# The tile transposed ahead, in more pieces: root, scaling with transposition, and each modulation by itself

## The chip, the cores and the metric

The kernel runs on one core of one Trainium2 chip. The metric is the device time of one execution in microseconds; the median of the runs is what counts. A core has five engines, each with its own queue of instructions that it works through in order: TensorE (PE, matrix products; PEld is its weight load), VectorE (DVE), ScalarE (ACT), GpSimd (POOL) and SyncE (SP), which here only issues DMA transfers (SPq in the rows). Engines wait for each other by semaphores.

## What is computed

One inference step of a hybrid decoder layer in float32: 2048 prompt tokens and 8 sample tokens, model width 1024. Cut to what matters here:

```python
ada = silu(c) @ w_ada + b_ada
shift, scale, gate = split(ada, 3)
hn = rmsnorm(x, g_norm) * (1.0 + scale) + shift
xa, za, q, k, v, glr, zg = split(hn @ w_in, SPLITS)
y_lru = rg_lru(conv4(xa)) * silu(za)
y_gla = rmsnorm(gla_chunked(q, k, v, decay(glr)), g_gla_norm) * silu(zg)
x = x + gate * (concat([y_lru, y_gla]) @ w_out)
y = rmsnorm(x, g_final)
```

`rmsnorm` scales a token's row by the inverse root of its mean square. The recurrence `rg_lru` has two sigmoid gates, each a block-diagonal product of the convolution's result; `gla_chunked` is a gated linear attention with 4 heads in chunks of tokens, whose running state passes from chunk to chunk.

## The kernel before

**Products.** Every float32 operand is kept as a high part (cast by ScalarE) and a low part (the rest, a subtraction on VectorE), and a product is three matmuls. A token tile is 128 tokens; the prompt is worked in two halves of 1024 tokens (`TH`). The normalised and transposed activations of a half lie in `hh` and `hl`.

**Stages of the first half.** The four heads run in the order 3, 0, 1, 2. For each, `values` makes the values in 8 token tiles (matmuls L388 to L390, 192 in all; ScalarE casts the high part at L999, VectorE makes the low part at L1000). Then come k and q (L703 to L705), the decay (matmul L1015, ScalarE L1020 to L1054, VectorE L1021 to L1051), the two decayed operands (L1063 for k, L1069 for q), their transposition on PE (L1084, L1087), and the chunks: VectorE L1088 to L1094, PE L1110 to L1118, the running state L1120 and L1121, the result copied out at L1124. ScalarE sums its squares (L167), VectorE takes the root and scales it (L1132), PE transposes it (L1206), VectorE multiplies by the silu gate (L1211; the silu itself is made at L1172 and L1173). Between the chunks run tiles of the recurrent group: convolution (ScalarE L1319, VectorE L1321), its high and low part (L1345, L1346), the two gates on PE (L1358 to L1360), their sigmoids (L1361), decay (L1366 to L1369) and recurrence (L1373 to L1377, results at L1395). Four accumulators of PE (`acc`) are shared by all of it, so PE can begin a fifth group only when the first has been read.

**Work for later, between these.** `weights` loads a piece of `w_in` (L340, two buffers), casts it (ScalarE L346), makes the low part (VectorE L347) and stores the pair for the second half (L364). `pair_weights` makes combinations of weights (VectorE L819, four a pair, then ScalarE L824 and VectorE L825). `out_weights` does the like for the output projection (L852 to L907). And `turn_ahead(q, gm)`, q from 0 to 7, makes the input of the second half: it loads 128 rows of the prompt (L266), ScalarE sums the squares of each row (L167, 128x1024), VectorE takes the inverse root in twelve small operations (L149 to L155), scales the rows (L183, 128x1024), transposes the tile in 32x32 blocks (L277, two of 128x512), multiplies by the modulation's scale and adds its shift (L284, twice 128x1024), and SyncE stores the result in four parts to `fd` (L289). `x` (the rows) and `w` (the transposed tile) share two buffers of one tag, `xt`. When one tile is stored, the next is started, so tile q+1 is loaded when tile q is done.

**What sets the order.** The program runs on a logical clock: `tick` is called once per block of matmuls, and `after(units, fn)` puts a piece of work on a heap, due that many ticks later; `tick` runs what is due. `behind(V)` makes the instructions of a piece follow VectorE's last one so far. In `turn_ahead` the square comes 3 ticks after the load; root, scaling and transposition together half a tick later; both modulations half a tick later; the stores half a tick later. The tile framework's scheduler then fixes the order on each engine from the program's order, the dependences and its own estimate of durations, so the order of an engine's queue is not the order of the code, and a piece that moves by a tick can change which instructions of other stages stand before it.

Of the kernel before, what the change touches and what calls it, by code (L numbers as in the profile page):

```python
# [8 lines left out]
F32 = mybir.dt.float32  # L9
# [3 lines left out]
OP = mybir.AluOpType  # L13

P = 128
D = 1024
KT = D // P
T = 2048
TH = T // 2
NS = 8  # L20
# [34 lines left out]
def hybrid_kernel(ctx, tc, i, o):  # L55
    nc = tc.nc
    V, S, G, PE, SP = nc.vector, nc.scalar, nc.gpsimd, nc.tensor, nc.sync
# [30 lines left out]
    xp = p1.enter_context(tc.tile_pool(name="xp", bufs=2))  # L88
# [52 lines left out]
                    mybir.DependencyClass.NoSync, mybir.DependencyReason.DATA), reason="in_order")  # L141
            last[x.engine] = x

    def rsqrt(pool, out, ss, n, rows, scale):

        y = pool.tile([P, 16], F32, tag="rs_y", name="rs_y", bufs=1)[:rows, :n]
        t = pool.tile([P, 16], F32, tag="rs_t", name="rs_t", bufs=1)[:rows, :n]
        x = pool.tile([P, 16], F32, tag="rs_x", name="rs_x", bufs=1)[:rows, :n]
        V.tensor_scalar(x, ss, scale, EPS, op0=OP.mult, op1=OP.add)  # L149
        V.tensor_scalar(t.bitcast(I32), x.bitcast(I32), 1, None, op0=OP.logical_shift_right)  # L150
        V.tensor_scalar(y.bitcast(I32), t.bitcast(I32), -1, 0x5F3759DF, op0=OP.mult, op1=OP.add)
        for it in range(3):
            V.tensor_tensor(t, y, y, op=OP.mult)
            V.scalar_tensor_tensor(t, t, -0.5, x, op0=OP.mult, op1=OP.mult)
            V.scalar_tensor_tensor(out if it == 2 else y, t, 1.5, y, op0=OP.add, op1=OP.mult)  # L155
# [13 lines left out]
    def squares(pool, xt, m=P, tag="f512", ss=None, j0=0):  # L169
        if ss is None:  # L170
            ss = pool.tile([P, 4], F32, tag="ss", name="ss", bufs=2)
        for j, x in enumerate(xt, j0):
            square_sum(pool, ss[:m, j:j + 1], x[:m], m, D, tag)
        return ss

    def scales(pool, ss, n, m=P):
        rs = pool.tile([P, 4], F32, tag="rs", name="rs", bufs=2)
        rsqrt(pool, rs[:m, :n], ss[:m, :n], n, m, 1.0 / D)
        return rs

    def times(xt, rs, m=P, j0=0):
        for j, x in enumerate(xt, j0):
            V.tensor_scalar(x[:m], x[:m], rs[:m, j:j + 1], None, op0=OP.mult)  # L183

    def normalize(pool, xt, m=P, tag="f512"):

        times(xt, scales(pool, squares(pool, xt, m, tag), len(xt), m), m)
# [74 lines left out]

    def turn_ahead(q, gm):

        x, w = [xp.tile([P, TH + NS], F32, tag="xt", name="xt")[:, :D] for _ in range(2)]
        SP.dma_start(x, i["x_prompt"][0, TH + q * P:TH + (q + 1) * P])  # L266

        def squared():
            ss = squares(xp, [x])
            after(0.5, lambda: scaled(ss))  # L270

        def scaled(ss):
            with behind(V):
                times([x], scales(xp, ss, 1))
                for h in range(2):
                    y, z = [v[:, 512 * h:512 * h + 512] for v in (w, x)]
                    V.transpose(y.rearrange("p (c k j) -> p c k j", c=4, k=4), z.rearrange("p (k c j) -> p c k j", c=4, k=4))  # L277
            after(0.5, modulated)

        def modulated():  # L280
            w3 = w.rearrange("p (b j) -> p b j", j=32)
            with behind(V):
                for n, op in enumerate((OP.mult, OP.add)):
                    V.tensor_tensor(w3, w3, gm[:, n, :, None].to_broadcast([P, 32, 32]), op=op)  # L284
            after(0.5, stored)

        def stored():
            for a in range(4):
                SP.dma_start(fd[q // 4, :, :, 4 * (q % 4) + a].rearrange("h (c r) f -> r (h c) f", c=4),  # L289
                             w[32 * a:32 * a + 32].rearrange("r (b f) -> r b f", b=8))  # L290
            if q < 7:
                turn_ahead(q + 1, gm)

        after(3, squared)

    def hn_load():

# [138 lines left out]
    rows = st.tile([NROW, D], F32, tag="rows", name="rows")  # L436
# [167 lines left out]
    def first_head():  # L604
# [158 lines left out]
    def ada_gate():  # L763

        pg = acc()

        def step(kt):
            ws = [xp.tile([P, TH + NS], F32, tag="xt", name="xt")[:, :D] for _ in range(2)]
            for n, w in enumerate(ws):
                SP.dma_start(w, i["w_ada"][0, (kt + n) * P:(kt + n + 1) * P, 2 * D:])  # L770

            def mm():
                for n in (1, 0):
                    for g in range(4):
# [12 lines left out]
        step(0)  # L787
# [339 lines left out]
    def gla_norm(nch, run):  # L1127
        _, on, ss = run
        rs = gp.tile([P, 4], F32, tag="ors", name="ors")
        rsqrt(gp, rs[:, :nch], ss[:, :nch], nch, P, 1.0 / DV)  # L1130
        for c in range(nch):
            V.tensor_scalar(on[:, c], on[:, c], rs[:, c:c + 1], None, op0=OP.mult)  # L1132
# [21 lines left out]
    def sample_out(h, qm, s0, done):  # L1154

        os_ = gp.tile([P, DV], F32, tag="os", name="os")
        po = psum.tile([P, 512], F32, tag="o", name="po", bufs=1)[:, :DV]
        for m in range(2):
            for n in (3, 0, 1, 2):
                PE.matmul(po[32 * n:32 * n + 32], qm[:, 4 * m + n], s0[m][:, n], start=m == 0, stop=m == 1)  # L1160
        for m in range(2):
            G.dma_start(o[7][0, 4 * m:4 * m + 4, h].rearrange("b k v -> k b v"), s0[m])
        V.tensor_copy(os_, po)
        ss = gp.tile([P, 4], F32, tag="oss2", name="oss2")
        rs = gp.tile([P, 4], F32, tag="ors2", name="ors2")
# [1051 lines left out]
    for n in range(2, 16):  # L2217
        g = n - 1
        x, prev = pairs[n], pairs[n - 1]
# [81 lines left out]
```

## Time and profile before

| what | value |
|---|---|
| median of 3 runs | 1453.01 us (1451.71 to 1453.09) |
| the profiled execution | 1452.74 us, its span 1450.5 us |
| granted TensorE clock, mean | 0.995 |
| busy: PE / DVE / ACT / POOL | 1418.1 / 1079.9 / 679.9 / 220.0 us |
| L284, VectorE, 128x1024 | 16 times, mean 1214 ns |
| L277, VectorE, 128x512 | 16 times, mean 689 ns |
| L183, VectorE, 128x1024 | 10 times, mean 752 ns (8 of them in `turn_ahead`) |
| L167, ScalarE, 128x1024 on `xt` | 10 times, mean 1055 ns (8 of them in `turn_ahead`) |

The eight tiles of `turn_ahead` run between 187 us (first load) and 488 us (last stores). In the rows of the timeline the first number is the start in microseconds from the span's start, the second the duration; then the engine, the line, the operation, `out<-in` by the program's names, shapes, and in brackets how long the engine sat idle before it and what it was waiting for. A row with `x8` joins eight neighbours. A row of windows gives the stretch, its length, the busy time of PE, PEld, DVE, ACT and POOL with the number of instructions, the granted clock, the DMA share and GB/s. A row of waits reads: engine, what it was about to do, what it waited for, then total, times and longest. Neighbouring VectorE rows overlap by some 0.08 us, so a row's share of the engine is its duration less that.

### The profile page before, as it was taken

How to read it: one execution, taken by the hardware profiler on the slowest of the kernel's cores; microseconds unless marked ns; L12 is line 12 of the kernel's file. 1: busy time of each engine (PE TensorE's matmuls, PEld its weight loads, DVE VectorE, ACT ScalarE, POOL GpSimd, SP SyncE). 2: the span in 40 equal slices, each digit the busy share in tenths (PEclk: the TensorE clock that was granted, in tenths of full speed). 3: DMA queues.
4: the chain of work that ended last, by engine and by line, in shares of the span. 5: the costliest groups of instructions: out<-in, count | busy, mean ns of one | idle time of the engine just before them, and what ended most of it. 6: DMA issues, size and time to landing. Idle time of an engine off the chain costs nothing.

```text
span 1450.5 us, 23542 instructions
## 1 busy us (share of the span) xinstructions
PE 1418.1 (98%) x8677; PEld 1246.9 (86%) x8677; DVE 1079.9 (74%) x2551; ACT 679.9 (47%) x1227; POOL 220.0 (15%) x362
## 2 busy tenths in 40 slices
PE   8999999989999999999999999999999999999998
PEld 6889989878888988888899999999998887778886
DVE  5757659877888768945458688596888986688886
ACT  4644544654366345524354454635567522144342
POOL 1200111121111114000110422333210000000000
PEclk9999999999999999999999999999999999999999
DMA  9755776885667667567744675665671767694453
GB/s 327 270 185 175 262 248 214 264 270 185 215 199 222 208 200 256 184 241 235 287 149 153 200 247 165 236 196 181 235 250 71 280 225 277 225 359 136 139 168 116
DMA packets 176840, 313.75 MB, mean 216 GB/s; under 512 B 20370, under 2 KB 106034, under 8 KB 173901
## 3 DMA queue, kind: packets, MB, share of 16 engines
q1 hardware_dynamic: 122821, 225.82, 46.0%
q0 software_dynamic: 22912, 70.96, 14.5%
q10 hardware_dynamic: 30992, 15.47, 3.6%
q8 instruction: 68, 1.11, 0.3%
q14 instruction: 47, 0.39, 0.1%
HBM read 192.74 MB, written 119.53 MB: 215 GB/s over the span
## 4 chain that ended last, share of the span: by engine, by line
PE 82%; DVE 9%; ACT 3%; DMA 3%; issue 2%; POOL 0%; DVEq 0%; SPq 0%; ACTq 0%
PE acc L1887 12%; PE acc L703 11%; PE acc L705 11%; PE acc L704 11%; PE tp L1887 9%; PE acc L1601 6%; PE acc L388 4%; PE acc L389 3%; PE acc L390 3%; PE po L1115 2%; DMA w<-parts 1%; DMA wada<-in_w_ada_dram 1%; PE acc L1358 1%; PE tp L1084 1%; PE tp L1206 1%
## 5 line engine op out<-in xcount | busy, mean ns | idle before, releaser
L703 PE MATMUL acc<-hh,w 128*128 128x512 f32 (+3 forms) x1112 | 378.0, 340 | 3.5 <-DVE zs L1173 1.9
L705 PE MATMUL acc<-hh,w 128*128 128x512 f32 (+3 forms) x1112 | 376.5, 339 | 0.0
L704 PE MATMUL acc<-hl,w 128*128 128x512 f32 (+3 forms) x1112 | 375.9, 338 | 0.0
L703 PEld LDWEIGHTS acc<-hh,w 128*128 128x128 f32 x1112 | 210.1, 189 | 21.3 <-issue 3.0
L705 PEld LDWEIGHTS acc<-hh,w 128*128 128x128 f32 x1112 | 210.0, 189 | 16.3
L704 PEld LDWEIGHTS acc<-hl,w 128*128 128x128 f32 x1112 | 210.0, 189 | 15.3
L1887 PE MATMUL acc<-w,a 128*128 128x512 f32 (+1 forms) x792 | 184.8, 387 | 0.0
L1887 PEld LDWEIGHTS acc<-w,a 128*128 128x128 f32 x792 | 146.8, 188 | 33.2 <-issue 3.4
L388 PE MATMUL acc<-w,hh 128*128 128x256 f32 (+1 forms) x508 | 145.0, 286 | 5.6 <-DVE vl L1000 5.4
L390 PE MATMUL acc<-w,hl 128*128 128x256 f32 (+1 forms) x508 | 143.5, 282 | 0.2 <-DVE hl L232 0.2
L389 PE MATMUL acc<-w,hh 128*128 128x256 f32 (+1 forms) x508 | 143.4, 282 | 0.0
L1887 PE MATMUL tp<-w,a 128*128 128x512 f32 x564 | 136.1, 391 | 0.0
L1887 PEld LDWEIGHTS tp<-w,a 128*128 128x128 f32 x564 | 105.2, 188 | 26.9 <-issue 5.2
L388 PEld LDWEIGHTS acc<-w,hh 128*128 128x128 f32 x508 | 96.5, 190 | 7.4 <-DVE vl L1000 6.0
L390 PEld LDWEIGHTS acc<-w,hl 128*128 128x128 f32 x508 | 96.6, 190 | 0.4 <-DVE hl L232 0.4
L389 PEld LDWEIGHTS acc<-w,hh 128*128 128x128 f32 x508 | 96.2, 189 | 0.2
L1172 ACT ACTIVATE zs<-acc 128x512 f32<-128x512 f32 (+3 forms) x70 | 34.3, 490 | 112.6 <-PE acc L705 105.7
L1737 ACT CAST a<-s 128x512 fp32r<-128x512 f32 x61 | 36.5, 620 | 94.7 <-issue 35.2
L1321 DVE SCALAR_TENSOR_TENSOR cv<-xa,vecT,cv 128x512 f32<-128x512 f32 (+2 forms) x120 | 76.2, 639 | 3.5 <-ACT cv L1319 2.9
L1173 DVE SCALAR_TENSOR_TENSOR zs<-zs,acc 128x512 f32<-128x512 f32 (+3 forms) x70 | 38.3, 548 | 35.6 <-ACT zs L1172 35.6
L999 ACT CAST vh<-acc 128x256 fp32r<-128x256 f32 x56 | 20.5, 370 | 87.6 <-PE acc L390 71.9
L1000 DVE TENSOR_TENSOR vl<-acc,vh 128x256 fp32r<-128x256 f32 x56 | 23.2, 418 | 47.0 <-ACT vh L999 46.9
(402 smaller groups left out, 2756.2 us busy)
## 6 DMA issues: line engine op xcount, KB each, us to landing
parts<-w SPq DMA_DIRECT2D x37, 1024.0 KB
w<-parts SPq DMA_DIRECT2D x28, 1024.0 KB
wr<-in_w_in_dram SPq DMA_DIRECT2D x38, 512.0 KB
a<-mixd SPq DMA_DIRECT2D x63, 256.0 KB
w<-wd SPq DMA_DIRECT2D x12, 1024.0 KB
w<-twd SPq DMA_DIRECT2D x20, 512.0 KB
wada<-in_w_ada_dram SPq DMA_DIRECT2D x16, 512.0 KB
mixd<-zs ACTq DMA_DIRECT2D x32, 256.0 KB
```

The source lines that it names most:

```text
L388: PE.matmul(ps, hh[:, kt, c], hi[:, kt % 4], start=kt == 0, stop=False)
L389: PE.matmul(ps, hh[:, kt, c], lo[:, kt % 4], start=False, stop=False)
L390: PE.matmul(ps, hl[:, kt, c], hi[:, kt % 4], start=False, stop=kt == KT - 1)
L703: PE.matmul(ps[:, :n], hi[:, kt], a, start=kt == 0, stop=False)
L704: PE.matmul(ps[:, :n], hi[:, kt], b, start=False, stop=False)
L705: PE.matmul(ps[:, :n], lo[:, kt], a, start=False, stop=kt == KT - 1)
L1172: S.activation(z, ps, AF.Tanh, scale=0.5)
L1173: V.scalar_tensor_tensor(z, z, 1.0, ps, op0=OP.add, op1=OP.mult)
L1321: V.scalar_tensor_tensor(cv[:, cq], xa[:, cq.start + k:cq.stop + k], cw[k], cv[:, cq], op0=OP.mult, op1=OP.add)
L1601: PE.matmul(ps, w[:, u, k], x[v][k], start=start and (k, u, v) == (0, 0, 0), stop=(k, u) == (3, 1), skip_group_check=True)
L1737: S.copy(t[:, 0, k], (low(t) if src is None else src)[:, k])
L1887: PE.matmul(ps, t[:, u, k], w[:, v, k, c], start=(q < 3 or ps is own) and (k, u, v) == (0, 0, 0), stop=(k, u) == (3, 1), skip_group_check= ...
```

## The change

`turn_ahead` is cut into more pieces: the square, then the root alone (`rooted`), then scaling and both transpositions (`turned`), then the multiplication, the addition (`modulated`, called twice) and the stores, each half a tick after the one before; the first delay is 3.5 ticks instead of 3. The buffer `w` is taken in `turned` instead of at the start, and the next tile's load is started right behind the transpositions instead of with the stores. `rsqrt` and `scales` get a parameter for the engine, with a branch for GpSimd that nothing calls. Every line number behind these places moves: in the changed kernel the low part of the values is L1011, L819 and L825 are L830 and L836, L284 is L297, L277 is L289, L183 is L189, the root is L149 to L161, the recurrence L1384 to L1388, L1063 and L1069 are L1074 and L1080, L858 is L869, L167 is L173, L999 is L1010, L346 is L357, L1020 is L1031.

```diff
     def turn_ahead(q, gm):
 
-        x, w = [xp.tile([P, TH + NS], F32, tag="xt", name="xt")[:, :D] for _ in range(2)]
+        x = xp.tile([P, TH + NS], F32, tag="xt", name="xt")[:, :D]
         SP.dma_start(x, i["x_prompt"][0, TH + q * P:TH + (q + 1) * P])
 
         def squared():
             ss = squares(xp, [x])
-            after(0.5, lambda: scaled(ss))
-
-        def scaled(ss):
+            after(0.5, lambda: rooted(ss))
+
+        def rooted(ss):
             with behind(V):
-                times([x], scales(xp, ss, 1))
+                rs = scales(xp, ss, 1)
+            after(0.5, lambda: turned(rs))
+
+        def turned(rs):
+            w = xp.tile([P, TH + NS], F32, tag="xt", name="xt")[:, :D]
+            with behind(V):
+                times([x], rs)
                 for h in range(2):
...
-            after(0.5, modulated)
-
-        def modulated():
+            if q < 7:
+                turn_ahead(q + 1, gm)
+            after(0.5, lambda: modulated(w, 0, OP.mult))
+
+        def modulated(w, n, op):
             w3 = w.rearrange("p (b j) -> p b j", j=32)
             with behind(V):
-                for n, op in enumerate((OP.mult, OP.add)):
-                    V.tensor_tensor(w3, w3, gm[:, n, :, None].to_broadcast([P, 32, 32]), op=op)
-            after(0.5, stored)
-
-        def stored():
+                V.tensor_tensor(w3, w3, gm[:, n, :, None].to_broadcast([P, 32, 32]), op=op)
+            after(0.5, (lambda: stored(w)) if n else lambda: modulated(w, 1, OP.add))
+
+        def stored(w):
             for a in range(4):
...
-            if q < 7:
-                turn_ahead(q + 1, gm)
-
-        after(3, squared)
+
+        after(3.5, squared)
```

Each engine has the same instructions before and after; what differs is the order, and on VectorE only in the part that runs between about 180 and 505 us. Three places, with the rows of the engine's queue.

VectorE in the second head's values, before, from just behind the first low part of the values (`vl`) to the second:

```order
L819 TENSOR_TENSOR tr<-tr 128x512
L1374 SCALAR_TENSOR_TENSOR tg<-xl,tg 128x1024
L819 TENSOR_TENSOR tr<-tr 128x512
L1375 TENSOR_TENSOR tx<-tx,tg 128x1024
L819 TENSOR_TENSOR tr<-tr 128x512
L1377 SCALAR_TENSOR_TENSOR tg<-xl,tx 128x1024
L284 TENSOR_TENSOR xt<-xt,gm 128x1024
L1380 COPY hc<-tg 128x1
L1395 SCALAR_TENSOR_TENSOR zs<-tg,zs 128x512
L284 TENSOR_TENSOR xt<-xt,gm 128x1024
L825 TENSOR_TENSOR tr<-tr,th 128x512 x2
L1000 TENSOR_TENSOR vl<-acc,vh 128x256
```

The changed kernel, at the same place: from the end of the tile's root (which follows the first low part) past the second and third low part to the fourth.

```order
L161 SCALAR_TENSOR_TENSOR rs<-rs_t,rs_y 128x1
L836 TENSOR_TENSOR tr<-tr,th 128x512
L1385 SCALAR_TENSOR_TENSOR tg<-xl,tg 128x1024
L836 TENSOR_TENSOR tr<-tr,th 128x512
L1386 TENSOR_TENSOR tx<-tx,tg 128x1024
L1011 TENSOR_TENSOR vl<-acc,vh 128x256
L1388 SCALAR_TENSOR_TENSOR tg<-xl,tx 128x1024
L1011 TENSOR_TENSOR vl<-acc,vh 128x256
L1391 COPY hc<-tg 128x1
L1406 SCALAR_TENSOR_TENSOR zs<-tg,zs 128x512 x2
L189 TENSOR_SCALAR xt<-xt,rs 128x1024
L1011 TENSOR_TENSOR vl<-acc,vh 128x256
```

The four L819 and the root have moved ahead of these rows, and scaling, transposition and modulations behind them; the second low part stands in front of the scan (L1377, now L1388) instead of behind both modulations.

VectorE in the second head's decay, before, from the last steps of a tile's root to L1069 (`xb`), which PE waits for; L1063 (`e<-acc,e`) stands just ahead of that root:

```order
L155 SCALAR_TENSOR_TENSOR rs_y<-rs_t,rs_y 128x1
L153 TENSOR_TENSOR rs_t<-rs_y 128x1
L154 SCALAR_TENSOR_TENSOR rs_t<-rs_t,rs_x 128x1
L155 SCALAR_TENSOR_TENSOR rs<-rs_t,rs_y 128x1
L183 TENSOR_SCALAR xt<-xt,rs 128x1024
L277 STREAM_TRANSPOSE xt<-xt 128x512 x2
L858 TENSOR_TENSOR g<-g,bt 128x512
L1069 SCALAR_TENSOR_TENSOR xb<-acc,xb 128x512
```

The changed kernel, from the last steps of the decay:

```order
L1062 TENSOR_TENSOR xb<-xb,mid 128x512
L1074 TENSOR_TENSOR e<-acc,e 128x512
L869 TENSOR_TENSOR g<-g,bt 128x512
L1080 SCALAR_TENSOR_TENSOR xb<-acc,xb 128x512
L1032 TENSOR_SCALAR xb<-acc,vecT 128x512
L1099 COPY_PREDICATED am<-mask,tp 128x512
L1035 TENSOR_TENSOR xb<-xb,e 128x512
L1105 TENSOR_TENSOR kTl<-tp,kTh 128x512
```

The root, the scaling and the transpositions are gone from between L1063 and L1069 (now L1074 and L1080) and stand behind the next decay.

ScalarE in the second head's values, before, from the square of a tile (`ss<-xt`, L167) to the start of the decay chain (L1020):

```order
L167 ACTIVATE junk,ss<-xt 128x1024
L999 CAST vh<-acc 128x256
L717 DMA mixd<-zs 128x4x128
L999 CAST vh<-acc 128x256
L824 CAST th<-tr 128x512 x2
L717 DMA mixd<-zs 128x4x128
L999 CAST vh<-acc 128x256 x2
L346 CAST w<-wr 128x1024
L999 CAST vh<-acc 128x256
L1020 ACTIVATE e<-acc,vecT 128x512
```

The changed kernel, with the square now at L173:

```order
L1010 CAST vh<-acc 128x256
L728 DMA mixd<-zs 128x4x128 x2
L1010 CAST vh<-acc 128x256 x2
L173 ACTIVATE junk,ss<-xt 128x1024
L1010 CAST vh<-acc 128x256
L357 CAST w<-wr 128x1024
L1010 CAST vh<-acc 128x256
L1031 ACTIVATE e<-acc,vecT 128x512
```

The square stood ahead of the last five high parts (`vh`), and stands ahead of the last two.

More of the change, by code (lines that the diff above doesn't have):

```diff
@@ L142, in in_order, with rsqrt @@
             last[x.engine] = x
-    def rsqrt(pool, out, ss, n, rows, scale):
+    def rsqrt(pool, out, ss, n, rows, scale, q=V):
         y = pool.tile([P, 16], F32, tag="rs_y", name="rs_y", bufs=1)[:rows, :n]
@@ L152, in rsqrt @@
         for it in range(3):
+            if q is G:
+                G.tensor_tensor(t, y, y, op=OP.mult)
+                G.tensor_tensor(t, t, x, op=OP.mult)
+                G.tensor_scalar(t, t, -0.5, 1.5, op0=OP.mult, op1=OP.add)
+                G.tensor_tensor(out if it == 2 else y, t, y, op=OP.mult)
+                continue
             V.tensor_tensor(t, y, y, op=OP.mult)
@@ L174, in squares, with scales @@
         return ss
-    def scales(pool, ss, n, m=P):
+    def scales(pool, ss, n, m=P, q=V):
         rs = pool.tile([P, 4], F32, tag="rs", name="rs", bufs=2)
-        rsqrt(pool, rs[:m, :n], ss[:m, :n], n, m, 1.0 / D)
+        rsqrt(pool, rs[:m, :n], ss[:m, :n], n, m, 1.0 / D, q)
         return rs
```

## The prediction

> **What bounds the kernel now.** I read the page first, then the waits of TensorE (PE), then the timelines of PE, VectorE (DVE), ScalarE (ACT) and SyncE's queue (SPq) around each wait.
>
> ```profile
> span 1450.5 us, 23542 instructions
> PE 1418.1 (98%) x8677; PEld 1246.9 (86%) x8677; DVE 1079.9 (74%) x2551; ACT 679.9 (47%) x1227; POOL 220.0 (15%) x362
> ```
>
> PE is busy for 98% of the span, so only a moment in which PE waits, or runs slowly, can be won or lost. The change reorders work between about 180 and 505 us. The view of waits on PE, for 200 to 500 us, has four entries:
>
> ```profile
> PE acc L388 <- DVE vl L1000: 5.4, 1, 5.4
> PE tp L1084 <- DVE xb L1069: 2.1, 1, 2.1
> PE acc L1358 <- ACT xh L1345: 0.4, 1, 0.4
> PE acc L1359 <- DVE xl L1346: 0.4, 1, 0.4
> ```
>
> I call them B (5.4), C (2.1) and A (the last two). B and C cost more than their waits. First B, as windows: the 192 value matmuls of the second head and of the third.
>
> ```profile
> 287.23:316.94 29.71, 24.29 (x194) 24.09 (x193) 22.14 (x43) 13.71 (x22) 6.64 (x12) 0.94 0.81 263
> 427.78:450.56 22.78, 22.78 (x194) 22.66 (x193) 18.68 (x39) 10.84 (x18) 5.73 (x10) 1.00 0.74 233
> ```
>
> The second head takes 29.71 us, the third 22.78: 6.9 lost, 5.4 in the wait and 1.5 in a granted clock of 0.94 instead of 1.00. PE's timeline shows where that clock goes, and the same at C:
>
> ```profile
> 306.95 0.58 PE L388 MATMUL acc<-w,hh 128*128 128x256 f32 x1 [5.42 <-DVE vl L1000]
> ...
> 332.94 1.16 PE L1084 MATMUL tp<-xb,e 128*128 128x128 f32 x8 [2.14 <-DVE xb L1069]
> ...
> 337.58 0.39 PE L703 MATMUL acc<-hh,w 128*128 128x512 f32 x1
> ...
> 188.73 1.16 PE L1084 MATMUL tp<-xb,e 128*128 128x128 f32 x8 [0.96 <-DVE xb L1069]
> ...
> 191.56 0.40 PE L703 MATMUL acc<-hh,w 128*128 128x512 f32 x1
> 191.79 0.39 PE L704 MATMUL acc<-hl,w 128*128 128x512 f32 x1
> ...
> 596.56 0.47 PE L703 MATMUL acc<-hh,w 128*128 128x512 f32 x1 [1.73 <-DVE zs L1173]
> ...
> 597.22 0.63 PE L705 MATMUL acc<-hh,w 128*128 128x512 f32 x1
> ```
>
> After 2.14, the stretch from L1084 to the eighth projection takes 4.64 (332.94 to 337.58); the same stretch after a wait of 0.96 takes 3.06 (188.73 to 191.79). So a slow stretch costs about 1.6; it also follows a wait of 1.73 (0.63 per matmul, where 0.39 is usual) and does not follow 0.96. C costs 3.7 in all.
>
> A sentence apart: the Trainium skill, "TensorE: Matmul & The Clock Gate", section "What's actually happening", says that the array falls to half clock after at least one idle window of about 3.4 us. By that only B would be followed by slow matmuls and no new wait below would, and the sum would come out 1.6 lower (about 1447.5). The rows at 596.56 and 332.94 disagree with it, so I do not take it.
>
> **What holds PE at B and C.** VectorE takes its instructions strictly in order. At B:
>
> ```profile
> 294.59 0.67 DVE L277 STREAM_TRANSPOSE xt<-xt 128x512 f32<-128x512 f32 x1
> 295.18 0.65 DVE L819 TENSOR_TENSOR tr<-tr 128x512 f32<-128x512 f32 x1
> 295.75 0.41 DVE L1000 TENSOR_TENSOR vl<-acc,vh 128x256 fp32r<-128x256 f32 x1
> ...
> 296.68 1.22 DVE L1374 SCALAR_TENSOR_TENSOR tg<-xl,tg 128x1024 f32<-128x1024 f32 x1
> ...
> 302.36 1.20 DVE L284 TENSOR_TENSOR xt<-xt,gm 128x1024 f32<-128x1024 f32 x1
> ...
> 305.27 1.28 DVE L825 TENSOR_TENSOR tr<-tr,th 128x512 f32<-128x512 f32 x2
> 306.48 0.41 DVE L1000 TENSOR_TENSOR vl<-acc,vh 128x256 fp32r<-128x256 f32 x1
> ...
> 296.47 0.35 ACT L999 CAST vh<-acc 128x256 fp32r<-128x256 f32 x1
> ```
>
> The second lower part of the values (L1000) runs at 306.48, though ACT had its input (L999) ready at 296.8: three more blocks of L819, the recurrence (L1374 to L1377), both modulations (L284) and two L825 stand ahead. It frees the accumulator that PE's sixth token tile needs. At C:
>
> ```profile
> 326.71 0.69 DVE L1063 TENSOR_TENSOR e<-acc,e 128x512 f32<-128x512 f32 x1 [0.70 <-ACT e L1053]
> 327.32 0.14 DVE L149 TENSOR_SCALAR rs_x<-ss 128x1 f32<-128x1 f32 x1
> ...
> 330.41 1.31 DVE L277 STREAM_TRANSPOSE xt<-xt 128x512 f32<-128x512 f32 x2
> 331.64 0.65 DVE L858 TENSOR_TENSOR g<-g,bt 128x512 f32<-128x512 f32 x1
> 332.21 0.68 DVE L1069 SCALAR_TENSOR_TENSOR xb<-acc,xb 128x512 f32<-128x512 f32 x1
> ```
>
> A whole tile's root (twelve small operations, 2.3), scaling (0.75) and transpositions (1.3) stand between L1063 and L1069, for which PE's L1084 waits.
>
> **The change part by part.** It adds and removes no instruction: each engine has the same ones as before, in another order. So all of it is waits.
>
> *The next load right behind the transposition.* Nothing by itself: SPq already issued it there (L266 at 295.29, in a fence below; the transposition that began at 294.59 ended at 295.26), ahead of the stores. What moves is what stands around it.
>
> *B.* In the new order the four L819, and a weight's lower part (L347), run ahead; behind the first L1000 come one L819, the root (2.3), two L825 (0.6 each), L1374 and L1375 (1.14 each; a row's time less the 0.08 by which neighbours overlap): 6.4 us, then the second L1000. The scan, scaling, transpositions and modulations follow, each behind one more L1000. The point to check is L347, now second in line; its weight is cast by ACT when the load has landed:
>
> ```profile
> 283.06 4.29 SPq L340 DMA_DIRECT2D wr<-in_w_in_dram  x2
> ...
> 291.74 1.05 ACT L346 CAST w<-wr 128x1024 fp32r<-128x1024 f32 x1 [2.34 <-DMA wr<-in_w_in_dram]
> ...
> 295.29 0.33 SPq L266 DMA_DIRECT2D xt<-in_x_prompt_dram  x1
> ...
> 300.85 1.06 ACT L167 ACTIVATE junk<-xt 128x1024 bf16<-128x1024 f32 x1 [1.69 <-DMA xt<-in_x_prompt_dram]
> ```
>
> That load took 8.7 us from issue (283.06 to 291.74), another of the same size 5.5 (295.29 to 300.85). The new order puts it behind one store instead of two, and its buffer is freed by a lower part (L347) that now runs earlier; adding durations along the queues it is issued at about 278.8, so it lands between 284.3 and 287.5; cast, L347, L819, L1373, L819 and the first L1000 end by 292.4, the second L1000 by 299.3. PE needs it at 301 (306.95 less 5.42, less what A gives). Margin 1.7: the whole of B goes, **-6.9**. If the load lands after 289.2, the margin is gone, and each further microsecond comes back.
>
> *C.* The root, scaling and transpositions move behind the chunk's work, and L1069 follows L858 directly: 4.3 earlier. Two things take from this. PE's L1084 now stands 8 projections earlier (0.23 each, 191.56 to 191.79: 1.8). And on ACT the square L167 of the next tile now stands between the sixth and seventh L999, and its load is issued only when the transpositions have ended, about 305.3 by the order above; with 5.5 it lands at 310.9. Behind L167 (1.1) queue an L999, a weight cast (L346, 1.05), the last L999 and L1020, the start of the decay chain:
>
> ```profile
> 317.24 0.69 ACT L1020 ACTIVATE e<-acc,vecT 128x512 f32<-128x512 f32 x1
> ```
>
> That start comes at 313.6, 3.6 earlier than now, where PE is 6.9 earlier. L1063 followed 9.5 behind; with 1.9 for L1063, L858 and L1069, L1084 can start at 325.0; PE is there at 330.8 - 6.9 - 1.8 = 322.1. Wait 2.9, slow stretch 1.6: 4.5 against 3.7 now. Bounds: if the load lands in time, L1020 runs at 310.2 and C goes wholly (-3.7); with 8.7 instead of 5.5 it is +4.0. I take the row of the same load: **+0.8**.
>
> *A.* Modulations and two convolution steps move behind L1346, and the gates' matmuls stand together: 0.44 and 0.39 of waits go, less some delay of L1345; 0.2 to 1.2, taken **-0.7**.
>
> *New waits.* Three places where a piece or its neighbour now stands ahead of something PE reads:
>
> ```profile
> 229.07 1.13 DVE L1132 TENSOR_SCALAR on<-on,ors 128x256 f32<-128x256 f32 x4
> ...
> 229.56 1.14 PE L1206 MATMUL tp<-ident,on 128*128 128x128 f32 x8
> ...
> 253.22 1.03 PE L1206 MATMUL tp<-ident,on 128*128 128x128 f32 x8
> ...
> 461.00 0.69 DVE L1063 TENSOR_TENSOR e<-acc,e 128x512 f32<-128x512 f32 x1 [0.70 <-ACT e L1053]
> 461.77 0.69 DVE L1069 SCALAR_TENSOR_TENSOR xb<-acc,xb 128x512 f32<-128x512 f32 x1
> ...
> 462.51 1.16 PE L1084 MATMUL tp<-xb,e 128*128 128x128 f32 x8
> ```
>
> D, the first: the tile's root, scaling, transposition and modulations leave the path of L1132, which ends about 226.2 instead of 230.1; but PE's L1206 moves 37 small projections ahead (0.12 each, as the values' 22.78 over 192), to about 225.0, and four L819 (0.6 each) now stand in the chunk's chain. Wait 0 to 1.6, taken **+0.9**. E, the second: two modulations (1.13 each) enter the chain of convolution and norm, and the norm's root is interleaved with a weight's lower part; L1132 ends 254.0 to 255, its first block is wanted at 253.3. 0 to 2, taken **+1.1**. F: one modulation stands between L1063 and L1069. L1069 ended at 462.46, just in time for 462.51, so 1.13 less that little slack is a wait of **+1.0**, or nothing if the modulation slips in earlier. All three are near the 0.96 that left the clock alone; a slow stretch would be 1.6 each.
>
> Elsewhere (365 to 400, the fourth head's values, SPq's weight loads, stores that now wait for later modulations) pieces move, but I find at least 0.7 of slack.
>
> **The sum.** -6.9 + 0.8 - 0.7 + 0.9 + 1.1 + 1.0 = -3.8. The profiled execution took 1452.74 (its span of 1450.5 and 2.2 around it), 0.27 below the median of 1453.01, so the median falls to about 1449.
>
> **Rivals.**
> 1. *All waits go* (A, B, C; no new one): 6.9 + 3.7 + 1.2 = 11.8, about 1441. For it: in the third head, where L1069 already follows L1063 (461.00, 461.77), L1084 has no wait. Against: the xt load stands ahead of the decay chain.
> 2. *The change does not do what it says: waits only move.* The new waits D, E, F each reach the length that costs the clock: +4.8, or D, E and C take their upper bounds (0.7 + 0.9 + 3.2): 1454. For it: 1.73 slows, and the place between 0.96 and 1.73 is unknown.
> 3. *Slower, by L347 at B.* If the weight load lands late, DVE stands still with every L1000 behind it. From 289.2 on B comes back; from about 294.6 (three microseconds later than it lands now) all 6.9 are back, the other terms stay (+3.1), and with the slow stretch of one new wait (1.6) it is 1457.5. For it: this load was the slowest, 8.7 us. Against: it is issued 4 us earlier with less ahead of it.
>
> **Chances.** Forecast 0.47; rival 1 0.10; rival 2 0.26; rival 3 0.17. A change under 0.2% (2.9 us) can't be told from none here, so faster means under 1450.1 and slower above 1455.9. The forecast lies near the first bound: faster 0.55, same 0.27, slower 0.18. Range 1442 to 1456: rival 1's edge to rival 2's.
>
> **What would show it.** Right: PE's wait for L1000 at the second head's values gone and that window near 22.8 us; a wait of about 3 for L1069 there, with ACT's L167 waiting for xt at about 311; waits near 1 for L1132 at 225 and 253, and for L1069 at 462. Wrong: a wait for L1000 with DVE standing at L347; matmuls of 0.41 or 0.63 behind a wait near 1; or a wait on any other line between 180 and 505.

## The result, and the profile after

| | kernel before | changed kernel |
|---|---|---|
| median of 12 runs | 1451.13 us (1448.39 to 1453.09) | 1442.48 us (1439.8 to 1447.22) |
| the profiled execution | 1452.74 us | 1446.12 us |

The ratio is 0.9947, with a 95% interval of 0.9938 to 0.9956: faster, and the medians lie 8.65 us apart where the sum gave 3.8. The page of the changed kernel, and below it its view of PE's waits between 180 and 515 us (in total, times, longest; us):

```profile
span 1444.3 us, 23546 instructions
PE 1415.9 (98%) x8677; PEld 1246.5 (86%) x8677; DVE 1081.8 (75%) x2551; ACT 678.9 (47%) x1227; POOL 220.9 (15%) x362
```

```profile
PE tp L1095 <- DVE xb L1080: 3.7, 3, 2.5
PE tp L1217 <- DVE on L1143: 0.8, 2, 0.5
```

The busy times are what they were. The waits for the values' low part (B) and for the gates' operands (A) are gone; L1095 is the former L1084, L1217 the former L1206. The second head's values as a window of the changed kernel, in the columns of the windows shown before:

```profile
288.16:310.94 22.78, 22.78 (x194) 22.78 (x193) 21.28 (x41) 10.76 (x18) 4.37 (x8) 1.00 0.85 289
```

The same 194 matmuls that took 29.71 us take 22.78, at a granted clock of 1.00: 6.93 us. PE's timeline has the waits that are left:

```profile
190.07 1.16 PE L1095 MATMUL tp<-xb,e 128*128 128x128 f32 x8 [0.96 <-DVE xb L1080]
...
226.90 1.14 PE L1217 MATMUL tp<-ident,on 128*128 128x128 f32 x8 [0.50 <-DVE on L1143]
...
255.60 0.44 PE L1217 MATMUL tp<-ident,on 128*128 128x128 f32 x2 [0.33 <-DVE on L1143]
...
325.51 1.47 PE L1095 MATMUL tp<-xb,e 128*128 128x128 f32 x8 [2.53 <-DVE xb L1080]
...
328.48 0.63 PE L716 MATMUL acc<-hh,w 128*128 128x512 f32 x1
...
457.22 1.16 PE L1095 MATMUL tp<-xb,e 128*128 128x128 f32 x8 [0.22 <-DVE xb L1080]
```

The first of them is the 0.96 us that was there before. Of these waits only the one of 2.53 (C) is followed by matmuls of 0.63. To see what each place was worth, I took the start of the same matmul in both timelines and subtracted. The difference is 1.36 us ahead of 225 (start-up, before the change begins) and changes at seven places up to 515 us, six that the prediction named and one that it did not:

| place | predicted | measured |
|---|---|---|
| D, L1217 at 226 | +0.9 | +0.42 |
| E, L1217 at 255 | +1.1 | +0.55 |
| A, gates up to 288 | -0.7 | -1.41 |
| B, second head's values | -6.9 | -6.93 |
| C, second head's L1095 | +0.8 | +0.40 |
| F, third head's L1095 | +1.0 | +0.34 |
| G, third head's L1217 at 491 | none | +0.48 |
| sum | -3.8 | -6.15 |

In this pair of profiles the six named places have the signs that were forecast, and each of the five terms other than B came out 0.4 to 0.7 us better than taken. G was missed: VectorE's L1143 comes 4.07 us earlier there (490.77 against 494.84) and PE 5.26 (491.00 against 496.26), so that PE catches up with its blocks.

The profiled executions lie 6.62 us apart, but the table does not show why to that accuracy. The start-up cost the changed kernel 1.36 us, and behind 515 us, where the order is the same, a load of weights for which PE had waited 1.32 us near 1010 us was in time; that wait comes and goes (0.46 in a second profile of the changed kernel, 1.50 and 0.71 in two of its variants). Nor is the pair typical: the profiled execution of the changed kernel lies 3.6 us above its median, that of the kernel before 1.6.

### The profile page after: what moved, and what is told of

Same layout as the page of the kernel before. It is cut to its first block, busy times and chain, and to the rows that moved or that the text cites. A ratio compares the mean times of both kernels' runs of the same rounds, so it can differ in the third digit from the quotient of the medians.

```text
span 1444.3 us, 23546 instructions
## 1 busy us (share of the span) xinstructions
PE 1415.9 (98%) x8677; PEld 1246.5 (86%) x8677; DVE 1081.8 (75%) x2551; ACT 678.9 (47%) x1227; POOL 220.9 (15%) x362
## 3 DMA queue, kind: packets, MB, share of 16 engines
q8 instruction: 68, 1.11, 0.3%
## 4 chain that ended last, share of the span: by engine, by line
PE 75%; DVE 9%; issue 6%; ACT 4%; DMA 4%; POOL 1%; SPq 0%; DVEq 0%; POOLq 0%; ACTq 0%
PE acc L1898 12%; PE acc L714 10%; PE acc L716 10%; PE acc L715 9%; PE tp L1898 9%; PE acc L1612 6%; PE acc L399 3%; PE acc L400 3%; PE acc L401 3%; PE po L1126 1%; DMA tr<-in_w_in_dram 1%; DMA twd<-tr 1%; PE acc L1369 1%; PE tp L1095 1%; PE tp L1217 1%
## 5 line engine op out<-in xcount | busy, mean ns | idle before, releaser
L1010 ACT CAST vh<-acc 128x256 fp32r<-128x256 f32 x56 | 20.7, 369 | 83.3 <-PE acc L401 63.3
L1011 DVE TENSOR_TENSOR vl<-acc,vh 128x256 fp32r<-128x256 f32 x56 | 23.4, 420 | 44.2 <-ACT vh L1010 44.0
```

## The experiments

The prediction hung on an order of instructions, and the change has three parts that each shift that order: the pieces, the earlier load and the longer first delay. Theory P ("phase") said that the gain is a matter of which instructions happen to fall between the first two low parts of the values, rival S ("split") that shorter pieces are what helps.

### The delay alone

```diff
 # kernel before
-        after(3, squared)
+        after(3.5, squared)
```

> The kernel before with one constant changed: the first delay of a tile is 3.5 ticks instead of 3; no piece is split and the next tile still starts with the stores. In VectorE's queue only one L819, two L825 and L1374 then stand between the first two low parts of the second head's values, and ScalarE's square of the next tile (L167) stands behind the decay's start. Theory P (phase): the gain of the change comes only from which instructions happen to fall between the first two low parts, so this kernel wins it too: PE's wait of 5.4 for L1000 and its slow stretch go (-6.9), and the wait at L1084 goes with them (-3.7) because no late load stands ahead of L1020; +0.4 for L1206 near 226. Ratio 0.992 to 0.994. Rival S (split): the pieces of their own or the earlier start are what frees VectorE; this kernel has neither, and keeps the wait of 5.4: ratio 0.999 to 1.001.

Measured: 1452.75 us, ratio 1.0017 (1.0006 to 1.0028). PE's waits, 180 to 515 us:

```profile
PE tp L1084 <- DVE xb L1069: 5.3, 3, 3.6
PE acc L1358 <- ACT xh L1345: 3.1, 1, 3.1
PE po L1115 <- DVE on L1124: 1.0, 1, 1.0
PE tp L1206 <- DVE on L1132: 0.5, 1, 0.5
PE acc L1359 <- DVE xl L1346: 0.4, 1, 0.4
PE acc L703 <- DVE vl L1000: 0.3, 1, 0.3
PE po L1118 <- DVE aml L1091: 0.2, 1, 0.2
```

No value matmul waits for L1000 (the 0.3 is the first projection behind them): with half a tick of delay and unsplit pieces B is gone. But a new wait of 3.1 stands at the gates, where the tile's root, scaling and transpositions now run ahead of the convolution (its first L1321 at 278.36, 274.41 before), and one of 3.6 at the third head. ScalarE's timeline has the cause of the second:

```profile
450.70 1.06 ACT L167 ACTIVATE junk<-xt 128x1024 bf16<-128x1024 f32 x1 [3.79 <-DMA xt<-in_x_prompt_dram]
...
452.01 0.69 ACT L1020 ACTIVATE e<-acc,vecT 128x512 f32<-128x512 f32 x1
```

The square L167 waits for its tile, and the third head's decay chain queues behind it. That is the mechanism forecast for C, at another head. P was right that B goes and wrong on the time: by the same subtraction of start times, 9.2 us were gained at B and C, and 9.6 lost at the gates and the third head and 1.7 at smaller places.

### The pieces without the delay

The earlier load stays, so this is the change less its delay.

```diff
 # changed kernel
-        after(3.5, squared)
+        after(3, squared)
```

> The changed kernel with the first square 3 instead of 3.5 units behind its load: the split and the early load without the delay, the counterpart of the run with the delay alone. Between the first two low parts L1011 VectorE now has one modulation, the scans and three subtractions, about 7.4 us, against 10.4 us in the kernel before and 6.5 us in the changed one (instruction times of the profile of before). Theory P (only what falls there counts): a wait of 0.5 to 2.5 us at the second head's values, 0.994 to 0.998. Rival S (the split itself is worth it, wherever it falls): no such wait, 0.992 to 0.995.

Measured: 1455.13 us, ratio 1.0032 (1.002 to 1.0043): slower than before, which neither theory gave. S falls. The wait for the second low part is back, 4.2 us, though what lies between the first two low parts came out as forecast (L1011, the former L1000, at 299.06 and 306.81: 7.75 us; 7.4 by the instructions). The forecast wait of 0.5 to 2.5 took the first low part as fixed; VectorE and PE show that it is not:

```profile
295.78 0.69 DVE L830 TENSOR_TENSOR tr<-tr 128x512 f32<-128x512 f32 x1 [5.73 <-issue]
...
299.06 0.42 DVE L1011 TENSOR_TENSOR vl<-acc,vh 128x256 fp32r<-128x256 f32 x1
...
306.81 0.40 DVE L1011 TENSOR_TENSOR vl<-acc,vh 128x256 fp32r<-128x256 f32 x1
...
307.26 0.39 PE L399 MATMUL acc<-w,hh 128*128 128x256 f32 x1 [4.21 <-DVE vl L1011]
```

VectorE stands idle for 5.73 us ahead of L830 (the former L819), with the low part queued behind it. L830 reads `tr`, a load that GpSimd issues. In this kernel, and then in the changed one:

```profile
288.92 0.90 POOL L826 DMA_DIRECT2D tr<-in_w_in_dram  x1 [7.31 <-issue]
```

```profile
282.15 0.89 POOL L826 DMA_DIRECT2D tr<-in_w_in_dram  x1 [5.55 <-issue]
...
289.43 0.69 DVE L830 TENSOR_TENSOR tr<-tr 128x512 f32<-128x512 f32 x1 [1.11 <-DMA tr<-in_w_in_dram]
...
293.51 0.42 DVE L1011 TENSOR_TENSOR vl<-acc,vh 128x256 fp32r<-128x256 f32 x1
...
300.12 0.42 DVE L1011 TENSOR_TENSOR vl<-acc,vh 128x256 fp32r<-128x256 f32 x1
```

L830 starts 6.9 and 7.3 us after the issue. GpSimd issues that load 6.8 us later in this kernel, and the first low part comes 5.55 us later. So B has two parts, when the first low part comes and what follows it. Why GpSimd issues the load later in this order was not traced.

What makes this kernel slower than the one before is mainly C. There the wait is 4.28 us instead of 2.14, and two slow stretches follow each other; this place alone loses 3.0 us. ScalarE's square stands inside the decay chain here and waits for a load that was issued at 316.44, 8.3 us earlier:

```profile
324.69 1.06 ACT L173 ACTIVATE junk<-xt 128x1024 bf16<-128x1024 f32 x1 [2.33 <-DMA xt<-in_x_prompt_dram]
...
333.68 1.65 PE L1095 MATMUL tp<-xb,e 128*128 128x128 f32 x6 [4.28 <-DVE xb L1080]
```

### Root, scaling and transposition in one piece

```diff
 # changed kernel
-            after(0.5, lambda: turned(rs))
+            turned(rs)
```

> The changed kernel with root, scaling and transposition in one piece again. Between the first two low parts of the second head's values now stand one modulation, the scan and their neighbours: some 8 us instead of 6.2, and the changed kernel's trace has 1.8 us of slack there (second low part ended 300.5, PE needed it at 302.3). Theory P: no wait of more than 0.6 for the low part; the square L167 falls behind the second high part, its load is early, so L1020 is not held and PE's wait at the second head's L1084 (2.5, and 1.6 of slow matmuls) is gone: ratio 0.990 to 0.993, faster than the changed kernel. Rival S: the root's own piece is needed; the wait for L1000 comes back by 2 us or more, ratio 0.996 or above.

Measured: 1450.91 us, ratio 0.9998 (0.9987 to 1.001). The values wait 1.46 us, and the second head's L1095 waits 3.70, because ScalarE stands at a late weight load inside the decay chain, between its first step (L1031 at 313.95) and its second (L1033):

```profile
318.56 1.05 ACT L357 CAST w<-wr 128x1024 fp32r<-128x1024 f32 x1 [3.91 <-DMA wr<-in_w_in_dram]
```

P's 0.990 to 0.993 was wrong. The number is S's, but not by S's mechanism: joining the piece brings back only 1.46 of the 5.42 us at B, under the 2 us that S asked for, and the larger wait comes from a load that is late in this order.

### The earlier load alone

```diff
 # kernel before
             with behind(V):
                 times([x], scales(xp, ss, 1))
...
+            if q < 7:
+                turn_ahead(q + 1, gm)
...
-            if q < 7:
-                turn_ahead(q + 1, gm)
```

`w` is taken where the scaling begins, as in the changed kernel; pieces and delay stay.

> The kernel before with one part of the change alone: the next tile is started right behind the transposition (its second buffer is taken there); root, scaling and transposition stay one piece, both modulations stay one piece, first delay 3. Between the first two low parts of the second head's values then stand scaling, transpositions, four L819, L1374, L1375, the scan and a modulation: some 11 us, against 10.4 before. Theory P: PE's wait for L1000 stays (4 to 6, with its slow stretch); the wait at L1084 is smaller or gone, since L1069 follows L858: ratio 0.997 to 1.000. Rival S: the early start is what gives the gain: ratio 0.994 to 0.996.

Measured: 1446.84 us, ratio 0.9976 (0.9967 to 0.9986), as P had it. C is down to 0.66 us, and B is longer than the 4 to 6 of the expectation. The trace shows less than the median: the profiled execution took 1450.27, and at 512 us its PE is only 0.7 us ahead of the kernel before. B's row:

```profile
308.30 0.58 PE L389 MATMUL acc<-w,hh 128*128 128x256 f32 x1 [7.57 <-DVE vl L1001]
```

Taken together, these kernels settle B (start times from the timelines of VectorE and PE, us; "values" is the first value matmul of the second head):

| kernel | values start | first low part | second low part | second, from values' start | PE's wait |
|---|---|---|---|---|---|
| before | 287.23 | 295.75 | 306.48 | 19.25 | 5.42 |
| changed | 288.16 | 293.51 | 300.12 | 11.96 | 0 |
| delay alone | 292.46 | 297.94 | 302.22 | 9.76 | 0 |
| pieces, no delay | 288.75 | 299.06 | 306.81 | 18.06 | 4.21 |
| root joined | 289.17 | 296.13 | 304.48 | 15.31 | 1.46 |
| earlier load alone | 286.44 | 296.16 | 307.83 | 21.39 | 7.57 |

In the four kernels that wait, the fifth column less the wait is 13.83, 13.85, 13.85 and 13.82. So PE can do without the second low part for 13.8 us; what comes later is wait, within 0.03 us. The changed kernel is 1.9 us inside. In the run with the delay alone the margin has two sources: the second low part comes 4.3 us earlier than in the kernel before, and the values, held up at the gates, start 5.2 us later. From a start at 287.23 that low part would come after 15.0 us, an estimated wait of 1.2. The pieces with the earlier load do not bring the gain at B without the delay; the pieces alone, and the delay with the earlier load, were not run.

### Both modulations in one piece, and the changed kernel again

```diff
 # changed kernel
-            after(0.5, lambda: modulated(w, 0, OP.mult))
+            after(0.5, lambda: modulated(w))
...
-                V.tensor_tensor(w3, w3, gm[:, n, :, None].to_broadcast([P, 32, 32]), op=op)
+                for n, op in enumerate((OP.mult, OP.add)):
+                    V.tensor_tensor(w3, w3, gm[:, n, :, None].to_broadcast([P, 32, 32]), op=op)
```

> The changed kernel with both modulations in one piece again. VectorE's order in the second head's values is that of the changed kernel row for row; in the third head no modulation stands between L1063 and L1069. Theory P: all of the gain stays and the wait of 0.2 to 0.4 at the third head's L1084 goes: ratio 0.993 to 0.995, the wait of 2.5 at the second head's L1084 stays. Rival S: the pair of modulations, 2.3 us in one piece, holds VectorE again somewhere: half of the gain or more is lost, ratio 0.997 or above.

Measured: 1440.53 us, ratio 0.9929 (0.9916 to 0.9941). B is gone, as P expected, and so is F; but C's 2.53 is gone too, which this edit does not touch: the order around L1031 (the former L1020) is the same. Its profile shows a load that was issued 1.7 us and landed 3.4 us sooner, and so it was run again, beside the changed kernel.

> Joined modulations once more, on the same chip as the changed kernel. If joining is better by itself: 0.992 to 0.994 of the kernel before and 1.5 to 2.5 us below the changed kernel beside it, again without a wait at the third head. If the difference of the first comparison was the luck of one load: within 1 us of the changed kernel.

> The changed kernel once more, beside its variants. If the third head's wait is set by the order of the instructions, it shows the same as before: 2.0 to 3.0 us for L1080 ahead of the third head's L1095, with the square L173 waiting 5 to 6 us for the load that is issued near 306.5. If it is set by how long that load happens to take (5.0 us in the first profile, 3.3 us in the kernel with joined modulations), the wait may be anything from 0 to 3 us in a second profile. Time 1441 to 1444 us, 0.994 to 0.996 of the kernel before.

Measured side by side: joined 1443.3 us, 0.9946 (0.9932 to 0.9959); changed 1444.18 us, 0.9952 (0.9939 to 0.9964). The difference shrank to less than can be told apart (the intervals overlap), and with joined modulations C's wait was 1.25 us in the second profile. ScalarE's square and the start of the decay chain, changed kernel first, then the first run of the joined one:

```profile
311.56 1.06 ACT L173 ACTIVATE junk<-xt 128x1024 bf16<-128x1024 f32 x1 [5.87 <-DMA xt<-in_x_prompt_dram]
...
314.08 0.70 ACT L1031 ACTIVATE e<-acc,vecT 128x512 f32<-128x512 f32 x1
```

```profile
308.16 1.06 ACT L173 ACTIVATE junk<-xt 128x1024 bf16<-128x1024 f32 x1 [2.99 <-DMA xt<-in_x_prompt_dram]
...
310.72 0.70 ACT L1032 ACTIVATE e<-acc,vecT 128x512 f32<-128x512 f32 x1
```

| profile | load issued | landed (square starts) | after | decay chain starts | PE's wait |
|---|---|---|---|---|---|
| changed | 306.55 | 311.56 | 5.0 | 314.08 | 2.53 |
| changed, again | 306.13 | 311.11 | 5.0 | 313.63 | 2.47 |
| joined | 304.82 | 308.16 | 3.3 | 310.72 | 0 |
| joined, again | 305.41 | 309.61 | 4.2 | 312.13 | 1.25 |

The chain starts 2.5 us behind the landing each time, and PE's wait follows it. This is theory C; what was open is whether the square only stands beside a late VectorE.

### The square moved out of the way

```diff
 # changed kernel
-        after(3.5, squared)
+        after(5.5 if q == 3 else 3.5, squared)
```

> The square of tile q = 3 alone comes 5.5 instead of 3.5 units after its load, which puts it on ScalarE behind L1031, L1033, L1034 of the third head instead of ahead of them; everything up to there is as in the changed kernel, the tiles behind it move by two units. Theory C (ScalarE holds L1031 because the square in front of it waits for the late load): L1031 comes near 311.6 instead of 314.08, the wait for L1080 ahead of the third head's L1095 goes from 2.5 to 0 to 0.5 us together with the 0.6 us matmuls behind it, and the shift from gate A's end to 345 us is better by 2 to 3.5 us; in all 0.992 to 0.9945 if the moved tiles cost nothing, up to 2 us more if the root's twelve steps now hold up another head. Rival (VectorE's backlog sets it, the square only stands beside it): L1031 comes at most 0.7 us earlier and 2 us or more of the wait stay; 0.9945 to 0.996.

Measured: 1441.35 us, ratio 0.9935 (0.9923 to 0.9948). L1031 starts 3.3 us earlier and nothing waits at the second head, so theory C holds and the rival falls:

```profile
310.49 0.37 ACT L1010 CAST vh<-acc 128x256 fp32r<-128x256 f32 x1 [0.36 <-PE acc L401]
310.76 0.70 ACT L1031 ACTIVATE e<-acc,vecT 128x512 f32<-128x512 f32 x1
```

The tiles behind it moved by two ticks, and at the third head all twelve steps of a root now stand between L1074 and L1080 (the former L1063 and L1069; L1074 starts at 450.64, L1080 at 453.44). That costs a wait of 1.29 us, within the "up to 2" of the expectation:

```profile
454.19 1.16 PE L1095 MATMUL tp<-xb,e 128*128 128x128 f32 x8 [1.29 <-DVE xb L1080]
```

So tile 4 was given 1.5 ticks, which puts all later tiles back where the changed kernel has them, with the modulations apart and joined:

```diff
 # changed kernel; and the one with joined modulations
-        after(3.5, squared)
+        after({3: 5.5, 4: 1.5}.get(q, 3.5), squared)
```

> As the run with the later square of tile q = 3 (5.5 units), but tile q = 4 takes 1.5 units, so that every tile behind it stands where it does in the changed kernel. Theory C: no wait at the third head's L1095 near 322 and none of the 1.3 us that the root's steps cost another head there; only the 0.2 us of the changed kernel near 455. 0.992 to 0.994 of the kernel before, 1 to 3 us below the changed one. Rival: what is gained at 322 comes back as another wait before 460, 0.994 to 0.996.

> The same with joined modulations. If the places are independent, the single wait ahead of 520 us that came with the change and is left is L1143 near 226 and 255 (0.3 to 0.5 each): 0.991 to 0.9935. If joining is worth nothing by itself: the same as the run beside it within 0.7 us.

Measured: 1440.67 us, 0.992 (0.9907 to 0.9934), and 1440.29 us, 0.9922 (0.9908 to 0.9935). PE's waits in the first of the two:

```profile
PE tp L1095 <- DVE xb L1080: 1.5, 3, 1.0
PE tp L1217 <- DVE on L1143: 0.7, 2, 0.4
```

Of the 1.5, 0.96 is the old wait at 190; 0.31 and 0.21 are left of C and F. With joined modulations those two are gone. Joining the modulations is worth nothing that can be measured. The changed kernel's ratio to the kernel before was 0.9947 (0.9938 to 0.9956) and, again, 0.9952 (0.9939 to 0.9964); 0.992 lies below both, with intervals that do not meet, though the two kernels were not run side by side. By that, two numbers for two tiles beat both kernels.

## Why the prediction was right, and where its sizes were off

Right by the range, and narrowly: 1442.48 is 0.5 us inside 1442 to 1456, and as a time it is nearer to rival 1's 1441 (all waits go) than to the forecast's 1449. That rival's mechanism is not what the trace shows, with 2.53 us at C and new waits at D, E and F. Of the 6.7 us between forecast and median, 1.9 are the starting point (1453.01 was the median of three runs, 1451.13 that of twelve), 2.4 the terms of the table; the other 2.5 belong to no place of the change that the pair of profiles shows.

**B.** Right to 0.03 us. The prediction let the first low part end by 292.4 and the second by 299.3; less the 0.93 by which the whole stage came later (288.16 against 287.23) they ended at 293.0 and 299.6, 0.6 and 0.3 late of a margin of 1.7. The feared weight load (rival 3) did not matter: ScalarE's cast of it ran at 287.49 without waiting, where it had waited 2.34 us before. The load that was close is another, `tr` from GpSimd's queue, for which VectorE waited 1.11 us. The prediction did not name it, and the run without the delay shows that 6.8 us more on it bring 4.2 us of B back. Rival 3 had the right shape and the wrong load.

**C.** Right in mechanism: it foretold the load's landing at 310.9 (311.56), L1020 at 313.6 (314.08) and a wait of 2.9 (2.53). Its bound "if the load lands in time, C goes wholly" was seen in the joined kernel. That the term and its sign fitted is luck all the same. In the second profile of the changed kernel the wait was 2.47, no slow stretch followed, and by the same subtraction C came to -1.3 instead of +0.40.

**D and E.** The step that failed is the end of L1132. The prediction worked with the end of the row of four blocks (226.2 and 254.0 to 255). Taken back by the shift ahead of each, 1.36 and 1.78, that row ended at 226.19 and 254.55: right. But PE's transpositions read the first block first. At D it ended at 226.76 and the fourth at 227.55, and PE started at 226.90; at E 255.54, 256.33 and 255.60. So the waits were 0.50 and 0.33 and the terms +0.42 and +0.55, not +0.9 and +1.1.

**F.** The modulation does stand between L1074 and L1080. VectorE's timeline:

```profile
454.74 0.69 DVE L1074 TENSOR_TENSOR e<-acc,e 128x512 f32<-128x512 f32 x1 [0.70 <-ACT e L1064]
455.35 1.22 DVE L297 TENSOR_TENSOR xt<-xt,gm 128x1024 f32<-128x1024 f32 x1
456.48 0.68 DVE L1080 SCALAR_TENSOR_TENSOR xb<-acc,xb 128x512 f32<-128x512 f32 x1
```

The prediction moved L1063 with PE; with PE's shift of -5.60 its 461.00 would be 455.40. It came at 454.74, 0.66 ahead of that, and what was left of the 1.13 was a wait of 0.22, in all +0.34. The step that failed is that it priced the place where the modulation went and not the one that it left. Before, both modulations and two weights' low parts stood ahead of L1024 in the same decay, so VectorE began L1024 0.71 us after ScalarE had ended its input (L1023). In the changed kernel one modulation is gone from there, VectorE waits for ScalarE, and L1035 (the former L1024) follows at once. Before, then changed:

```profile
455.75 0.63 ACT L1023 ACTIVATE e<-e 128x512 f32<-128x512 f32 x1
...
457.09 0.68 DVE L1024 TENSOR_TENSOR xb<-xb,e 128x512 f32<-128x512 f32 x1
```

```profile
450.81 0.69 DVE L1035 TENSOR_TENSOR xb<-xb,e 128x512 f32<-128x512 f32 x1 [1.45 <-ACT e L1034]
```

**A.** Taken -0.7, came -1.41, beyond its bounds of 0.2 to 1.2. The waits of 0.44 and 0.39 explain 0.83; the rest is overlap that a wait takes away. Matmuls of 0.39 us start 0.23 apart when nothing holds them. Before, starts around the two waits lay 0.83 and 0.33 apart (277.44, 278.27, 278.60) and 0.79 and 0.33 (279.30, 280.09, 280.42), in all 1.36 more than four times 0.23. The kernel before:

```profile
277.44 0.39 PE L705 MATMUL acc<-hh,w 128*128 128x512 f32 x1
278.27 0.73 PE L1358 MATMUL acc<-xh,wg 128*128 128x512 f32 x2 [0.44 <-ACT xh L1345]
...
280.09 0.50 PE L1359 MATMUL acc<-xl,wg 128*128 128x512 f32 x1 [0.39 <-DVE xl L1346]
280.42 0.40 PE L1360 MATMUL acc<-xh,wg 128*128 128x512 f32 x1
```

In the changed kernel the six gate matmuls start 0.23 apart from 280.00 on. The sum had priced these waits by their length alone.

**The load and the slack.** The prediction put the earlier load at "nothing by itself". Alone it cut C from 2.14 to 0.66, lengthened B from 5.42 to 7.57, and the median fell by 4.0 us. And "at least 0.7 of slack" elsewhere did not hold at G.

**The whole.** The five named terms other than B all came on the better side of what was taken, and G was not in the sum. The rival in which waits only move, given 0.26, did not come true here; it did in the run with the delay alone, where what was gained at B and C came back at two other places, and in the run without the delay.

## What to carry to other kernels

In an in-order queue next to a full TensorE, cost what stands in front of each awaited instruction, and also what the instructions in front wait for: a load on another engine's queue decided B as much as the row of instructions did. When a piece of work is cut or delayed, all later pieces of its chain shift with it, and each new neighbourhood is a new price; so move one piece and put the rest back (here tile 3 later, tile 4 sooner by as much), and price the place that it leaves as well as the one where it goes. Where several blocks feed a consumer that starts with the first, price the first block's end.

## What was unexpected of the hardware

**The slow stretch of the clock depends on more than the length of the wait.** The changed kernel waited 2.53 us at C in one profile and 2.47 in the other. From L1095 to the sixth projection behind it the first took 4.19 us (325.51 to 329.70), the second 2.58 (325.06 to 327.64), since its projections ran at 0.39:

```profile
325.06 1.16 PE L1095 MATMUL tp<-xb,e 128*128 128x128 f32 x8 [2.47 <-DVE xb L1080]
...
327.64 0.39 PE L716 MATMUL acc<-hh,w 128*128 128x512 f32 x1
```

Behind the wait of 4.21 in the run without the delay the matmuls ran at full pace for about 1.1 us (from 307.26) and only then fell back (0.29 at 307.49, 0.41 at 308.54).

The twelve traces show a pattern. Every slow stretch between 100 and 1430 us has a granted clock of 0.50, lasts 3.41 us or a multiple, and within one trace all lie on one grid of 3.41 us. What counts is how long PE stood idle in the grid step before. Windows of one step each (length, PE's busy time first; 1.00 or 0.50 is the granted clock) show it in the changed kernel, and then in its second profile, where the grid, placed by that trace's slow stretch at 590.35, cuts the wait of 2.47 in two:

```profile
322.80:326.21 3.41, 0.88 (x7) 0.70 (x7) 2.62 (x5) 3.23 (x5) 0.00 (x0) 1.00 1.05 384
326.21:329.62 3.41, 3.41 (x14) 3.02 (x13) 2.44 (x5) 2.89 (x5) 0.00 (x0) 0.50 0.80 237
```

```profile
320.70:324.11 3.41, 1.89 (x9) 1.20 (x7) 2.68 (x9) 1.84 (x4) 0.00 (x0) 1.00 1.02 416
324.11:327.53 3.42, 2.47 (x17) 2.30 (x18) 2.83 (x5) 3.36 (x6) 0.00 (x0) 1.00 1.12 348
```

At full clock, a step with 2.07 us idle or more was always followed by a slow one, a step with 1.62 or less never, and steps with 1.72 to 1.86 were in two of eight cases. The wait of 1.73 from which the prediction took its threshold is there in all twelve traces (1.72 to 1.73); in four a slow stretch follows (the kernel before, the changed kernel twice, the earlier load alone), in eight none. So whether a wait of 1.7 to 2.5 us costs 1.6 us more depends on where it falls in the grid, and that differs from one execution to the next; the prediction's threshold was the reading of one trace.

The Trainium skill, "TensorE: Matmul & The Clock Gate", section "What's actually happening", says that activity is watched in a free-running window of 3413 ns. The grid agrees with it. Its rule that one idle window is needed does not: 2.53 us is shorter, and was enough once.

**The same 512 KB load landed after 3.3 to 8.3 us.** The four rows of the table above give 3.3 to 5.0 for tile 3. In the run with the delay alone another tile's load was issued at 444.56 and read at 450.70; in the run without the delay one issued at 316.44 was read at 324.69, and with the earlier load alone one issued at 283.52 was read at 291.86, each time by a ScalarE that stood waiting for it. Where such a load stands ahead of a chain that PE waits for, that spread alone is worth over 2 us of a run.
